# Remainders of the weights on VectorE: seven block products, the sums of their weights, and the order around the output projection

## The chip, the cores and the metric

The kernel runs on one core of one Trainium2 chip, in one launch. Its time is the device time of that launch in microseconds (us), and lower is better. "Before" is the kernel as it stood, "after" is the kernel with the change below; both compute the same outputs from the same inputs.

## The reference

One layer of a streaming encoder, on 1024 rows of 1024 columns, all in float32. Its parts, cut to what matters:

```python
mod = (silu(c) @ ada_w + ada_b)          # six vectors: shift, scale, gate, twice
h = rmsnorm(x, pre_norm_mix) * (1 + scale_m) + shift_m
q_lat, kv_lat, k_idx, w_idx, z, xbc, dt_raw, g_a, g_b = split(h @ w_in)
y_a = sparse_mla_attention(...) @ w_o_attn
y_b = ssd_mixer(z, xbc, dt_raw, ...) @ w_o_ssd          # 2048 -> 1024
mix = (sigmoid(g_a) * y_a + sigmoid(g_b) * y_b) @ w_out
x = x + gate_m * rmsnorm(mix, post_norm_mix)
h2 = rmsnorm(x, pre_norm_ffn) * (1 + scale_f) + shift_f
u_gate, u_up = split(h2 @ w_ffn_in)                     # 2 x 2816 columns
x = x + gate_f * rmsnorm((silu(u_gate) * u_up) @ w_ffn_out, post_norm_ffn)
```

ssd_mixer is a Mamba-2 scan: a causal convolution of four taps over xbc, softplus of dt_raw, a scan in chunks, and at its end rmsnorm(y * silu(z), ssd_norm). sparse_mla_attention scores the keys with a small indexer, keeps the best 256, and attends to these.

## The kernel before

**Precision.** A float32 operand is used as two halves: "hi", a copy rounded to TensorE's fast float32 format (made by ScalarE, for weights at L155), and "lo", the remainder src - hi (for weights at L156, `wlo`). One product of 128x128 weights with 128x512 data is three matmuls: hi by hi, hi by lo, lo by hi. So every tile of weights costs one instruction of ScalarE and one subtraction, and TensorE waits for both.

**Weights.** `Stream W` brings them in tiles of 128x512 (four blocks of 128x128) in the order in which they are planned: a load on SP's queue into `wraw` (4 buffers), `whi` (3) and `wlo` (3). A tile is loaded and split two tiles ahead of its use. In before every `wlo` is made by GpSimd.

**Buffers.** Four arenas of 128x512 tiles: H (32), Q (26), R (8, of twice the size), EV (9). A tile is free when its last reader is done.

**Order.** The Tile scheduler orders the instructions of each engine by a simulated timeline; only in sections under `in_order` TensorE's order is that of the code. So an instruction that is handed to another engine, or written elsewhere, moves its neighbours on every engine.

**Stages**, in the time of the profiled execution: the projection w_in (from the start on, with the convolutions of xbc and the gates z), attention (660 to 1110 us lie wholly in it), the scan's end and the projection of attention, then the products of w_o_ssd (1437 to 1669 us, matmuls at L1625), w_out in two halves (L1416, ahead of the last products and behind them), and the feed-forward part (L1694 and on).

**The seven products.** w_o_ssd, 2048 by 1024, and the normed y are cut into 2x2 blocks, and the result is formed of seven products of half size in place of eight. `SEQ` and `SEQ1` list them as (i, c): product i (1 to 7) for column tile c (0 to 3), 24 matmuls each, two tiles of weights. Products 4 to 7 need sums of weight blocks. `ssd_sums` forms these ahead of time and stores them in DRAM (`d_s`): 8 units, each four loads, four additions or subtractions on GpSimd (L1029 to L1032) and four stores; before, they are called in the projection phase (`SUMS_AT`, and in the first two groups of the convolution), on four buffers `sum_bufs` (`adaw` and `vt` in the traces).

`ssd_step` runs one (i, c): its `tasks` first (sums of y: `both_sums`, `last_sum`, `third_sum`, `plain`), then 24 matmuls, then the addition of the result in PSUM (`pos`) to the partial sums. A sum of y is split by `y_parts` into `yh` (ScalarE) and `yw` (the remainder, L1258, or L1261 where it is scaled). `merge_out` joins a finished column tile with the gates in four steps: multiply by the gate (L1403), add the attention's part (L1404), hi (ScalarE, L1406), lo (L1407); w_out reads the result, `mg`. Rows of the output have two halves of 512, b = 0 and b = 1; `mixed(b)` is w_out for half b, eight column tiles of 24 matmuls. `residual_steps(0)`, the norm and residual of half 0 (`mix`, `sqm`, `xr`, h2), is spread over the last products and `mixed(1)`. Its row norms are L276 (spread by TensorE) and L270 (GpSimd).

Before, the order on TensorE is: 22 products, `mixed(0)`, six products, `mixed(1)`:

```python
SEQ = [(i, c) for i in (1, 2, 6, 5, 3) for c in range(4)] + [(7, 0), (7, 1)]
SEQ1 = [(4, 0), (7, 2), (4, 1), (7, 3), (4, 2), (4, 3)]
```

**Feed-forward.** `gate_up(t)` forms tile t of both halves of w_ffn_in, again by block products with weights' sums; `w_parts` splits a tile (ScalarE L1686, GpSimd L1687). The last two tiles before `EARLY` are "held": part of their work is done earlier and finished later; a rule of the code (`ends`) keeps one of these products behind another on TensorE.

**Attention's side work.** `ada_next()` is called again and again beside attention. It brings the columns of ada_w for the modulation vectors (two loads, then GpSimd's L326 and L327 on `adaw`) and a few late items. GpSimd also makes the masks `nm` there (L803) and `r` (L864).

## Time and profile before

| | |
|---|---|
| runs | 2388.24, 2385.63, 2382.94 us; median 2385.63 |
| profiled execution | 2381.24 us, its span 2379.5 us (1.7 us lie around it) |
| granted TensorE clock, mean | 0.990 |
| ScalarE, busy | 1217.8 us, 51% of the span |
| HBM | 304.84 MB read, 107.24 MB written, 173 GB/s over the span |
| GpSimd's `wlo` (L156) over the whole span | 238 instructions, 332.3 us, 1.40 us each |
| GpSimd's `wr` (L1687, two forms together) | 151 instructions, 217.9 us |
| between 660 and 1110 us: GpSimd's L803, L326, `wlo`, L327 | 74.7, 55.1, 36.5, 34.8 us |

How to read the rows that follow. The profile is of one execution on the chip. PE is TensorE's matmuls, PEld its weight loads, DVE is VectorE, ACT ScalarE, POOL GpSimd, SP the queue that issues DMAs. A row of a group names the line, the engine, the operation, what it writes and reads by the program's names, shapes, and the count; then busy time and the mean of one in ns; then idle time of the engine just ahead, and what ended it. A row of the instructions in time begins with the start and the duration in us. A row of waits reads: engine, its instruction, `<-` the instruction or DMA that released it, and total us, times, longest. "PEclk" is the granted clock as a share of full speed.

### The profile page before, as it was taken

The numbers are of one execution on the slowest core, as the hardware profiler recorded it, in microseconds if no ns is written. First come the engines' busy times: TensorE is split into PE (matmuls) and PEld (weight loads), VectorE is DVE, ScalarE is ACT, GpSimd is POOL, SyncE is SP. The second block draws the span as 40 slices with busy tenths as digits, with TensorE's granted clock in tenths as the row PEclk, the third lists the DMA queues.
The fourth block names the chain that finished last, engine by engine and source line by source line (L and its number), as shares of the span: only waits on it lengthen the run. The fifth ranks groups of instructions, "written<-read, shape, count | busy, mean of one in ns | idle before, by whom it ended". The sixth has DMA issues, their size and how long they took to land. (4 is left out here: it accounts for less than half of the span.)

```text
span 2379.5 us, 35122 instructions
## 1 busy us (share of the span) xinstructions
PE 2317.4 (97%) x11736; PEld 1893.8 (80%) x11736; DVE 1650.6 (69%) x3040; ACT 1217.8 (51%) x2362; POOL 1233.2 (52%) x947
## 2 busy tenths in 40 slices
PE   9999999999999999999999998999999999999997
PEld 5878888888888888888887776788788788888886
...
GB/s 268 153 232 247 195 174 163 196 89 97 99 80 85 98 89 100 98 90 144 224 239 287 292 251 281 211 176 208 89 274 137 132 161 149 162 94 282 208 194 165
DMA packets 251716, 411.27 MB, mean 173 GB/s; under 512 B 25568, under 2 KB 93328, under 8 KB 251536
## 3 DMA queue, kind: packets, MB, share of 16 engines
...
HBM read 304.84 MB, written 107.24 MB: 173 GB/s over the span
## 5 line engine op out<-in xcount | busy, mean ns | idle before, releaser
L156 POOL TENSOR_TENSOR wlo<-wraw,whi 128x512 fp32r<-128x512 f32 x238 | 332.3, 1399 | 371.4 <-ACT whi L155 340.8
L1694 PE MATMUL p<-xh,wr 128*128 128x512 f32 x880 | 273.6, 391 | 3.2 <-DVE g L1785 3.0
L155 ACT ACTIVATE whi<-wraw 128x512 fp32r<-128x512 f32 x238 | 148.7, 627 | 211.8 <-issue 52.5
L1687 POOL TENSOR_TENSOR wr<-a,wr 128x512 fp32r<-128x512 f32 x107 | 153.7, 1451 | 94.1 <-ACT wr L1686 61.9
L1694 PEld LDWEIGHTS p<-xh,wr 128*128 128x128 f32 x880 | 165.9, 189 | 38.5 <-DVE g L1785 3.4
L1694 PE MATMUL p<-xl,wr 128*128 128x512 f32 x440 | 171.8, 390 | 0.0
L252 POOL TENSOR_TENSOR fwl<-fw,fwh 128x512 fp32r<-128x512 f32 (+1 forms) x78 | 108.2, 1398 | 103.1 <-ACT fwh L251 70.5
L326 POOL TENSOR_TENSOR adaw<-adaw,cs 128x512 f32<-128x512 f32 x64 | 68.1, 1065 | 153.2 <-DMA adaw<-ada_w 116.5
L856 ACT ACTIVATE lg<-lg,mx 128x256 f32<-128x256 f32 (+7 forms) x128 | 99.1, 774 | 57.4 <-DVE mx L853 57.2
L1686 ACT ACTIVATE wr<-a 128x512 fp32r<-128x512 f32 x107 | 65.9, 628 | 114.5 <-PE p L1694 84.4
L651 DVE SCALAR_TENSOR_TENSOR acc<-rel,widx,acc 128x384 f32<-128x384 f32 (+2 forms) x90 | 106.7, 1208 | 15.2 <-ACT rel L646 14.9
L1694 PE MATMUL p<-h2h,wr 128*128 128x512 f32 x352 | 110.4, 391 | 1.7 <-ACT xh L251 1.4
L701 ACT ACTIVATE junk<-acc,cand__2216 128x1024 bf16<-128x1024 f32 (+2 forms) x96 | 86.3, 898 | 39.5 <-DVE cand__2216 L744 31.2
L646 ACT ACTIVATE rel<-prel 128x512 f32<-128x512 f32 (+3 forms) x160 | 77.0, 523 | 45.9 <-PE prel L645 42.6
L1625 PE MATMUL pos<-yh,wlo 128*128 128x512 f32 x224 | 90.2, 403 | 8.7 <-POOL wlo L156 8.6
L1694 PEld LDWEIGHTS p<-xl,wr 128*128 128x128 f32 x440 | 83.0, 189 | 17.3
L1687 POOL TENSOR_TENSOR wr<-s,wr 128x512 fp32r<-128x512 f32 x44 | 64.2, 1463 | 61.0 <-ACT wr L1686 56.2
L1625 PE MATMUL pos<-yh,whi 128*128 128x512 f32 x224 | 90.1, 402 | 1.4 <-ACT whi L155 1.0
L699 DVE TENSOR_SCALAR_CACHE_REDUCE junk<-acc,cand__2225 128x896 bf16<-128x896 f32 (+2 forms) x96 | 88.5, 922 | 1.5
L1625 PE MATMUL pos<-yw,whi 128*128 128x512 f32 x224 | 89.1, 398 | 0.0
L853 DVE CUSTOM_DVE_ANT_0 lg<-plg,nm 128x256 f32<-128x256 f32 (+1 forms) x128 | 51.5, 404 | 52.9 <-PE plg L844 52.3
L1416 PE MATMUL pot<-mg,whi 128*128 128x512 f32 x256 | 80.6, 396 | 3.6 <-ACT whi L155 3.4
...
## 6 DMA issues: line engine op xcount, KB each, us to landing
wraw<-w_in SPq DMA_DIRECT2D x129, 256.0 KB, 2.8
a<-w_ffn_in SPq DMA_DIRECT2D x122, 256.0 KB, 3.2
al<-d_a SPq DMA_DIRECT2D x88, 256.0 KB, 4.3
yl<-d_y SPq DMA_DIRECT2D x72, 256.0 KB, 3.9
adaw<-ada_w SPq DMA_DIRECT2D x64, 256.0 KB, 2.9
...
d_a<-g SPq DMA_DIRECT2D x42, 256.0 KB, 2.3
...
```

The costliest lines, as they stand in the source:

```text
L155: self.hi = behind(S.activation(hi[:, :kt], raw[:, :kt], AF.Copy))
L156: self.lo = behind(G.tensor_tensor(lo[:, :kt], raw[:, :kt], f(hi[:, :kt]), op=OP.subtract))
L252: (lo_eng or V).tensor_tensor(lo, src, f(hi), op=OP.subtract)
L646: S.activation(rel[:, 512 * b:512 * b + w_], pr[:, 0:w_], AF.Relu)
L651: V.scalar_tensor_tensor(acc[i][:, 0:n], rel[:, 0:n], ws, acc[i][:, 0:n], op0=OP.mult, op1=OP.add)
L699: V.tensor_scalar(jk, y, a_, 0.0, op0=op, op1=OP.add, accum_out=o)
L701: S.activation(jk, y, AF.Sign, scale=-1.0, bias=a_, accum_out=o)
L856: S.activation(lg[:, 0:n], lg[:, 0:n], AF.Exp, scale=-1.0, bias=m, accum_out=rr[:, 2 * t + hh:2 * t + hh + 1])
L1416: T.matmul(o, wt[:, k % 4, :], xs[k][xi][0], start=first and n == 0 and i == 0, stop=last and n == len(ks) - 1 and i == 2)
L1625: T.matmul(p, w[k // 4][wi][:, k % 4], YO[i][k][xi], start=start and k == 0 and n == 0, stop=k == SK - 1 and n == 2, skip_group_check=True)
L1687: G.tensor_tensor(w[:, 1], src, f(w[:, 0]), op=OP.subtract)
L1694: ins.append(T.matmul(p, w[:, wi, i], X[x][i][xi], start=start and i == 0 and k == 0, stop=i == 3 and k == 2, skip_group_check=True).ins)
```

## The change

1. **Remainders of weights.** `Stream W` gets a list of engines, `eng`. It is GpSimd as before, VectorE while `SEQ` runs, and from the first w_out on VectorE and GpSimd by turns.
2. **Sums and merges of the products.** The remainders of y for products 3 and 5, the subtraction in `third_sum`, and the addition in `merge_out` are all on VectorE; before, GpSimd had some or all of them.
3. **Products ahead of w_out.** `SEQ` now has 26 products, `SEQ1` two. Six merges of half 1 are done by `merge_later` during `mixed(0)`, with buffers of H and Q; the last two follow their products. `residual_steps(0)` is handed out in other places, and one multiply-add of h2 goes to ScalarE.
4. **Sums of the weights.** `ssd_sums` becomes a generator, called from `ada_next()`: a step is one instruction of GpSimd with its store, a unit has three EV tiles (`wsum`), and all of it lies beside attention. The projections no longer have it.
5. **Feed-forward.** `w_parts` of the two held tiles are on VectorE, and the rule `ends` is dropped.

```diff
         def load(self):
...
-            self.lo = behind(G.tensor_tensor(lo[:, :kt], raw[:, :kt], f(hi[:, :kt]), op=OP.subtract))
+            self.lo = behind(self.eng[len(self.tiles) % len(self.eng)].tensor_tensor(lo[:, :kt], raw[:, :kt], f(hi[:, :kt]), op=OP.subtract))
...
     def ada_next():
+        next(sums, None)
...
+    def ssd_sums():
+        for c in range(4):
+            for k0 in (0, 4):
+                x, y, z = (EV("wsum", (P, 4, P)) for _ in range(3))
...
+                load(x, c, 0)
+                load(y, 4 + c, 0)
+                load(z, 4 + c, SK)
+                yield
+                G.tensor_tensor(x, y, x, op=OP.subtract)
+                store(0, x)
+                yield
+                G.tensor_tensor(y, z, y, op=OP.subtract)
+                store(2, y)
+                yield
+                G.tensor_tensor(z, x, z, op=OP.subtract)
+                store(1, z)
+                load(x, c, SK)
+                yield
+                G.tensor_tensor(x, x, z, op=OP.add)
+                store(3, x)
...
     def conv_group(g):
...
-            elif g or i > 1:
-                ssd_sums(*next(s_units))
...
-    def merge_out(t, b, src, sb, ld, eng=V):
+    def merge_out(t, b, src, sb, ld, where=None):
         V.tensor_tensor(sb, src, sb, op=OP.mult)
-        eng.tensor_tensor(sb, sb, ld, op=OP.add)
-        hi, lo = in_r("mg")
+        V.tensor_tensor(sb, sb, ld, op=OP.add)
+        hi, lo = (where("mg", dt=F32R), where("mg", dt=F32R)) if where else in_r("mg")
...
+            if b == 0:
+                behind_merge(S.activation(h2, h2, AF.Identity, bias=mod[:, 24 + t:25 + t], scale=am2[:, t:t + 1]))
+            else:
+                behind_merge(V.tensor_scalar(h2, h2, am2[:, t:t + 1], mod[:, 24 + t:25 + t], op0=OP.mult, op1=OP.add))
...
-    SEQ = [(i, c) for i in (1, 2, 6, 5, 3) for c in range(4)] + [(7, 0), (7, 1)]
-    SEQ1 = [(4, 0), (7, 2), (4, 1), (7, 3), (4, 2), (4, 3)]
+    SEQ = [(i, c) for i in (1, 2, 6, 5, 3, 7) for c in range(4)] + [(4, 0), (4, 1)]
+    SEQ1 = [(4, 2), (4, 3)]
...
-            y_parts(5, k, y21, H_, eng=G)
+            y_parts(5, k, y21, H_)
...
-            y_parts(3, k, s2, H_, eng=(V, G)[k % 2])
+            y_parts(3, k, s2, H_)
...
-            (G if k % 2 else V).tensor_tensor(x[0], x[0], x[1], op=OP.subtract)
+            V.tensor_tensor(x[0], x[0], x[1], op=OP.subtract)
...
+    def merge_later(t):
+        x = merge_in(t, 1)
+        merge_gate(1, x[0])
+        merge_out(t, 1, u4s[t - 4] if t > 3 else u2s[t], *x, where=Q if t > 3 else H_)
...
+        W.eng[:] = [V]
         for n, x in enumerate(SEQ):
             ssd_step(x, (SEQ + SEQ1)[n + 1])
...
-        out = []
+        out, W.eng[:] = [], [V, G]
         for t, _ in enumerate(mixed(0, MG[0], out)):
-            load, work = next(plains)
-            work(load())
+            if t < 6:
+                merge_later((4, 5, 6, 7, 0, 1)[t])
         rest = residual_steps(0, *out, x1, 2)
         for n, x in enumerate(SEQ1):
             ssd_step(x, (SEQ1 + [None])[n + 1])
-            if n < 4:
-                next(rest)
+            next(rest)
         out = []
         for t, _ in enumerate(mixed(1, MG[1], out)):
-            if t in (0, 2, 3):
+            for _ in range((3, 0, 1, 1, 0, 0, 0, 0)[t]):
                 next(rest)
...
+        parts_eng[0] = V if t in held else G
...
-        if t == EARLY - KEPT + 1:
-            tc.add_manual_dep(ends[0], j.name, mybir.DependencyInfo(
```

After's lines are numbered 14 to 16 higher in this part of the code: L1258 is L1272, L1403 to L1407 are L1417 to L1421, L1642 is L1657.

Where the instructions stand on an engine, at three places. A row has the line, the operation and what it writes from what it reads, with the buffers' numbers. The first is GpSimd at the start of the products (1437 us in before). `zy` is the last product of y with the gate z; `wlo` and `yw` are remainders of weights and of y. Before:

```order
L1226 TENSOR_TENSOR zy_14693<-zy_14693 128x512
L156 TENSOR_TENSOR wlo_14881<-wraw_14879,whi_14880 128x512
L156 TENSOR_TENSOR wlo_14922<-wraw_14920,whi_14921 128x512
L1258 TENSOR_TENSOR yw_14954<-yl_14936,yh_14953 128x512
L1258 TENSOR_TENSOR yw_15020<-yl_14961,yh_15019 128x512
L156 TENSOR_TENSOR wlo_14928<-wraw_14926,whi_14927 128x512
L1258 TENSOR_TENSOR yw_15089<-yl_15027,yh_15088 128x512
L156 TENSOR_TENSOR wlo_14971<-wraw_14969,whi_14970 128x512
L156 TENSOR_TENSOR wlo_15037<-wraw_15035,whi_15036 128x512
L1258 TENSOR_TENSOR yw_15161<-yl_15096,yh_15160 128x512
L156 TENSOR_TENSOR wlo_15043<-wraw_15041,whi_15042 128x512
```

After the change, GpSimd at the same place (`wlo_16391` is a weight of w_out, 26 products on):

```order
L1240 TENSOR_TENSOR zy_14717<-zy_14717 128x512
L156 TENSOR_TENSOR wlo_14905<-wraw_14903,whi_14904 128x512
L156 TENSOR_TENSOR wlo_14946<-wraw_14944,whi_14945 128x512
L156 TENSOR_TENSOR wlo_14952<-wraw_14950,whi_14951 128x512
L270 TENSOR_TENSOR r_15033<-v_15031,nhalf_96 128x4
L270 TENSOR_TENSOR r_15174<-v_15172,nhalf_96 128x4
L156 TENSOR_TENSOR wlo_16391<-wraw_16389,whi_16390 128x512
```

And VectorE after the change, a little later in the same section (`yl` and `s2` are sums of y, `ya` the attention's projection):

```order
L1321 SCALAR_TENSOR_TENSOR ya_14909<-ya_14909,poa_14911 128x512
L1272 TENSOR_TENSOR yw_15113<-yl_15051,yh_15112 128x512
L156 TENSOR_TENSOR wlo_14995<-wraw_14993,whi_14994 128x512
L1272 TENSOR_TENSOR yw_15109<-s2_15105,yh_15108 128x512
L1275 SCALAR_TENSOR_TENSOR yw_15117<-yl_15057,vec_87,yh_15116 128x512
L1560 SCALAR_TENSOR_TENSOR yl_15120<-yl_15122,vec_87,yl_15120 128x512
L156 TENSOR_TENSOR wlo_15061<-wraw_15059,whi_15060 128x512
L1566 TENSOR_TENSOR s2_15105<-yh_14750,yl_15120 128x512
L1272 TENSOR_TENSOR yw_15185<-yl_15120,yh_15184 128x512
```

The remainders of weights and of y have left GpSimd's row and stand between VectorE's own sums of y.

The second place is VectorE after the last product, up to the last remainder of a merge (`mg`), which the second w_out needs last. `mk4` is that product's sum; `mix` and `xr` belong to the norm and residual of half 0. Before:

```order
L1469 TENSOR_TENSOR mix_16510<-mix_16510,mix_16462 128x512
L1404 TENSOR_TENSOR sgb_16761<-sgb_16761,yal_16762 128x512
L1469 TENSOR_TENSOR mix_16558<-mix_16558,mix_16510 128x512
L1407 TENSOR_TENSOR mg_16862<-sgb_16761,mg_16862 128x512
L1642 TENSOR_TENSOR mk4_14932<-pos_16777,mk4_14932 128x512
L1403 TENSOR_TENSOR sgb_16819<-mk4_14932,sgb_16819 128x512
L1404 TENSOR_TENSOR sgb_16819<-sgb_16819,yal_16820 128x512
L1407 TENSOR_TENSOR mg_16905<-sgb_16819,mg_16905 128x512
```

VectorE after the change, the rows that end with the last `mg`:

```order
L1417 TENSOR_TENSOR sgb_16790<-mk4_14956,sgb_16790 128x512
L1478 SCALAR_TENSOR_TENSOR mix_16636<-mix_16636,gm_14938,prn_16888 128x512
L1478 SCALAR_TENSOR_TENSOR mix_16689<-mix_16689,gm_14938,prn_16888 128x512
L1478 SCALAR_TENSOR_TENSOR mix_16742<-mix_16742,gm_14938,prn_16888 128x512
L1478 SCALAR_TENSOR_TENSOR mix_16784<-mix_16784,gm_14938,prn_16888 128x512
L1479 TENSOR_TENSOR xr_16895<-mix_16477,xr_16895 128x512
L1479 TENSOR_TENSOR xr_16899<-mix_16583,xr_16899 128x512
L1418 TENSOR_TENSOR sgb_16790<-sgb_16790,yal_16791 128x512
L1479 TENSOR_TENSOR xr_16907<-mix_16689,xr_16907 128x512
L1483 TENSOR_TENSOR mix_16477<-mix_16477,mix_16425 128x512
L156 TENSOR_TENSOR wlo_16957<-wraw_16955,whi_16956 128x512
L1421 TENSOR_TENSOR mg_16885<-sgb_16790,mg_16885 128x512
```

The four steps of the last merge stood together; now steps of the residual and a remainder of w_out's weights stand between them, five more instructions ahead of L1417 (four of `mix`, one of `wlo`) not shown.

The third place is GpSimd in the first projections, with the weights' sums in before (L1029 to L1032):

```order
L156 TENSOR_TENSOR wlo_3178<-wraw_3176,whi_3177 128x512
L1029 TENSOR_TENSOR adaw_2831<-adaw_2832,adaw_2831 128x512
L1030 TENSOR_TENSOR adaw_2832<-vt_2833,adaw_2832 128x512
L1031 TENSOR_TENSOR vt_2833<-adaw_2831,vt_2833 128x512
L270 TENSOR_TENSOR r_858<-v_856,nhalf_96 128x4
L1032 TENSOR_TENSOR vt_2833<-vt_2833 128x512
L156 TENSOR_TENSOR wlo_3184<-wraw_3182,whi_3183 128x512
L156 TENSOR_TENSOR wlo_3269<-wraw_3267,whi_3268 128x512
```

After the change these sums stand on GpSimd beside attention (L1039 to L1049), among the masks and the columns of ada_w:

```order
L326 TENSOR_TENSOR adaw_7123<-adaw_7123,cs_134 128x512
L327 TENSOR_TENSOR adaw_7122<-adaw_7122,adaw_7123 128x512
L1039 TENSOR_TENSOR wsum_6950<-wsum_6951,wsum_6950 128x512
L156 TENSOR_TENSOR wlo_7032<-wraw_7030,whi_7031 128x512
L1042 TENSOR_TENSOR wsum_6951<-wsum_6952,wsum_6951 128x512
L326 TENSOR_TENSOR adaw_7279<-adaw_7279,cs_134 128x512
L1045 TENSOR_TENSOR wsum_6952<-wsum_6950,wsum_6952 128x512
```

A unit's four instructions have moved from one run in the projections to single places beside attention, each behind its own loads.

More of the change, by code (lines that the diff above doesn't have):

```diff
@@ L44 @@
 SK = 8
-SUMS_AT = range(2)
 COLS = {}
@@ L142, in __init__ @@
             self.tag, self.width, self.bufs = tag, width, (raw_bufs, hi_bufs, lo_bufs)
+            self.eng = [G]
         def plan(self, items):
@@ L1019, in weight_sums, with load, store @@
             SP.dma_start(d_t[i, c][:, k0:k0 + n], x)
-    s_units = iter([(c, k0) for c in range(4) for k0 in (0, 4)])
-    def ssd_sums(c, k0):
-        b11, b12, b21, b22 = sum_bufs
-        for x, t, o in ((b11, c, 0), (b12, 4 + c, 0), (b22, 4 + c, SK), (b21, c, SK)):
-            tc.add_manual_dep(SP.dma_start(x, a["w_o_ssd"][t][:, o + k0:o + k0 + 4]).ins, W.issue, mybir.DependencyInfo(
-                mybir.DependencyClass.NoSync, mybir.DependencyReason.DATA), reason="behind")
-        G.tensor_tensor(b11, b12, b11, op=OP.subtract)
-        G.tensor_tensor(b12, b22, b12, op=OP.subtract)
-        G.tensor_tensor(b22, b11, b22, op=OP.subtract)
-        G.tensor_tensor(b21, b21, b22, op=OP.add)
-        for i, x in enumerate((b11, b22, b12, b21)):
-            SP.dma_start(d_s[i, c][:, k0:k0 + 4], x)
+    def ssd_sums():
+        for c in range(4):
+            for k0 in (0, 4):
+                x, y, z = (EV("wsum", (P, 4, P)) for _ in range(3))
+                def load(d, t, o):
+                    tc.add_manual_dep(SP.dma_start(d, a["w_o_ssd"][t][:, o + k0:o + k0 + 4]).ins, ada_after[0], mybir.DependencyInfo(
+                        mybir.DependencyClass.NoSync, mybir.DependencyReason.DATA), reason="behind")
+                def store(i, d):
+                    SP.dma_start(d_s[i, c][:, k0:k0 + 4], d)
+                load(x, c, 0)
[14 more added lines that the diff above has]
+                store(3, x)
+    sums = ssd_sums()
     def conv_group(g):
-        for i, t in enumerate(group_tiles(g)):
+        for t in group_tiles(g):
             conv_out(conv(*t))
@@ L1600, in build @@
         tasks[3, c] = [third_sum(5 + c, H_)] * (c < 3) + [gates_of(4 + c, 0)]
-        tasks[7, c] = [gates_of(4 + c, 1)]
-        tasks[4, c] = [gates_of(c, 1)]
-    plains = iter([plain(4, k, 1) for k in range(SK)])
+        tasks[7, c] = [plain(4, 2 * c, 1), plain(4, 2 * c + 1, 1)]
+        tasks[4, c] = [] if c < 2 else [gates_of(c, 1)]
     loaded = {}
@@ L1636, in ssd_step @@
         elif i == 3:
-            merge_out(4 + c, 0, p, *gates[4 + c, 0], eng=G)
+            merge_out(4 + c, 0, p, *gates[4 + c, 0])
         elif i == 7:
             V.tensor_tensor(u4s[c], p, u4s[c], op=OP.add)
-            merge_out(4 + c, 1, u4s[c], *gates[4 + c, 1], eng=G)
         else:
             V.tensor_tensor(u2s[c], p, u2s[c], op=OP.add)
-            merge_out(c, 1, u2s[c], *gates[c, 1])
+            if c > 1:
+                merge_out(c, 1, u2s[c], *gates[c, 1])
+    def merge_later(t):
+        x = merge_in(t, 1)
+        merge_gate(1, x[0])
+        merge_out(t, 1, u4s[t - 4] if t > 3 else u2s[t], *x, where=Q if t > 3 else H_)
     def ry(b):
@@ L1682, in w_load @@
         return r
+    parts_eng = [G]
     def w_parts(src):
@@ L1686, in w_parts @@
         S.activation(w[:, 0], src, AF.Copy)
-        G.tensor_tensor(w[:, 1], src, f(w[:, 0]), op=OP.subtract)
+        parts_eng[0].tensor_tensor(w[:, 1], src, f(w[:, 0]), op=OP.subtract)
         return w
     def product(p, w, x, start):
-        ins = []
         for i in range(4):
             for k, (wi, xi) in enumerate(P3):
-                ins.append(T.matmul(p, w[:, wi, i], X[x][i][xi], start=start and i == 0 and k == 0,
-                                    stop=i == 3 and k == 2, skip_group_check=True).ins)
-        return ins
+                T.matmul(p, w[:, wi, i], X[x][i][xi], start=start and i == 0 and k == 0, stop=i == 3 and k == 2,
+                         skip_group_check=True)
     def first_two(a11, a12):
@@ L1706, in first_two @@
         return p, p1, p2
-    held, lower_n, sum_n, ahead, ends = {}, [0], [0], [None], [None]
+    held, lower_n, sum_n, ahead = {}, [0], [0], [None]
     def sum_tile(name):
@@ L1786, in gate_up @@
         p5 = bank("p5")
-        j = product(p5, w_parts(s1), "1", True)[-1]
-        if t == EARLY - KEPT + 1:
-            tc.add_manual_dep(ends[0], j.name, mybir.DependencyInfo(
-                mybir.DependencyClass.NoSync, mybir.DependencyReason.DATA), reason="behind")
+        product(p5, w_parts(s1), "1", True)
         u1 = EV("u1")
@@ L1804, in gate_up @@
         SP.dma_start(d_a[t][:, half(1)], g1)
-        ends[0] = product(p, w_parts(a22), "4", False)[0]
+        product(p, w_parts(a22), "4", False)
         if p1 is None:
```

3 lines of the change are left out of this document (removed).

## The prediction

> **What bounds the kernel now.** I read the page first, then the busy times by stage, the engines' waits, and single instructions in time.
>
> ```profile
> span 2379.5 us, 35122 instructions
> PE 2317.4 (97%) x11736; PEld 1893.8 (80%) x11736; DVE 1650.6 (69%) x3040; ACT 1217.8 (51%) x2362; POOL 1233.2 (52%) x947
> ```
>
> TensorE (PE) is busy 97% of the span, so only what makes it wait, or run at a lower clock, can be won. The view by stretches (busy us, instructions begun, granted clock, DMA share) says where that is:
>
> ```profile
> core 0: us, PE busy (x) PEld busy (x) DVE busy (x) ACT busy (x) POOL busy (x), PEclk, DMA share, GB/s
> ...
> 160.00:180.00 20.00, 14.91 (x59) 11.96 (x58) 13.92 (x25) 5.15 (x7) 10.57 (x8) 0.83 0.62 223
> ...
> 660.00:1110.00 450.00, 446.06 (x2879) 371.91 (x2879) 315.59 (x932) 243.71 (x502) 220.34 (x211) 1.00 0.28 91
> ...
> 1437.00:1530.00 93.00, 79.24 (x325) 61.29 (x324) 88.60 (x81) 42.38 (x77) 68.88 (x44) 0.94 0.79 257
> 1530.00:1633.00 103.00, 103.00 (x456) 85.27 (x456) 38.01 (x40) 44.83 (x77) 58.95 (x45) 1.00 0.49 162
> 1633.00:1669.00 36.00, 35.23 (x158) 28.05 (x156) 30.11 (x36) 15.49 (x27) 26.62 (x19) 1.00 0.69 246
> 1669.00:1722.00 53.00, 47.96 (x205) 38.20 (x206) 32.51 (x40) 24.25 (x43) 30.09 (x22) 0.97 0.27 90
> ...
> 1820.00:1880.00 60.00, 55.40 (x235) 44.72 (x234) 40.12 (x43) 21.02 (x38) 38.11 (x27) 0.97 0.39 126
> ```
>
> The fed stretch 1530 to 1633 gives TensorE's pace: 103/456 = 0.226 us a matmul. Against it (length minus count times 0.226) the others lose: 160-180 (call it C) 6.7 us; 1437-1530 (A, the first products) 19.6; 1633-1669 0.3; 1669-1722 (B, the second w_out) 6.7; 1820-1880 (E, the first feed-forward tiles) 6.9. The change touches the causes of all of them; together they are 40 us. TensorE's own waits there (total, times, longest):
>
> ```profile
> PE pos L1625 <- POOL wlo L156: 8.6, 8, 2.1
> PE prn L276 <- POOL r L270: 3.5, 1, 3.5
> ...
> PE pot L1416 <- ACT whi L155: 3.4, 2, 2.9
> ...
> PE p L1694 <- DVE g L1785: 3.0, 1, 3.0
> ...
> PE pw L231 <- DVE cv L988: 5.6, 3, 5.1
> ```
>
> In A, TensorE waits for remainders of weights (wlo) that GpSimd (POOL) makes; in C for a convolution tap of VectorE (DVE). Why are they late? Instructions in time around 1445, 1486 and 1536:
>
> ```profile
> 1445.18 0.69 DVE L1550 TENSOR_TENSOR s<-yw,s 128x512 f32<-128x512 f32 x1
> 1445.78 0.69 DVE L1258 TENSOR_TENSOR yw<-s,yh 128x512 fp32r<-128x512 f32 x1
> ...
> 1485.32 1.75 DVE L1258 TENSOR_TENSOR yw<-s,yh 128x512 fp32r<-128x512 f32 x1
> 1486.99 1.77 DVE L1562 SCALAR_TENSOR_TENSOR s<-yl,vec,s 128x512 f32<-128x512 f32 x1
> 1488.69 1.77 DVE L1258 TENSOR_TENSOR yw<-s,yh 128x512 fp32r<-128x512 f32 x1
> ...
> 1497.12 0.68 DVE L1630 TENSOR_TENSOR vt<-pos,vt 128x512 f32<-128x512 f32 x1
> ...
> 1486.48 1.73 POOL L1258 TENSOR_TENSOR yw<-yl,yh 128x512 fp32r<-128x512 f32 x1
> 1488.17 1.74 POOL L1258 TENSOR_TENSOR yw<-s,yh 128x512 fp32r<-128x512 f32 x1
> ...
> 1536.01 1.30 POOL L156 TENSOR_TENSOR wlo<-wraw,whi 128x512 fp32r<-128x512 f32 x1 [1.43 <-ACT whi L155]
> ```
>
> VectorE's remainder (L1258) takes 0.69 us and follows its neighbour by 0.60 at 1445, but 1.75 to 1.77 with starts 1.70 apart at 1486, where GpSimd works at the same step: 1.69 apart and 1.73 each, against 1.30 alone. The two take turns: a turn of 1.70 holds one VectorE instruction (0.61) and one of GpSimd (so 1.09). L1630, with one input in PSUM, takes 0.68 while GpSimd works. GpSimd's work in A, by groups:
>
> ```profile
> L156 POOL TENSOR_TENSOR wlo<-wraw,whi 128x512 fp32r<-128x512 f32 x26 | 40.3, 1559 | 17.0 <-ACT whi L155 15.5 <-issue 1.4
> L1258 POOL TENSOR_TENSOR yw<-yl,yh 128x512 fp32r<-128x512 f32 x8 | 13.2, 1670 | 2.0 <-ACT yh L1257 2.0
> L1258 POOL TENSOR_TENSOR yw<-s,yh 128x512 fp32r<-128x512 f32 x4 | 6.6, 1639 | 2.9 <-DMA wraw<-d_s 2.9
> L1570 POOL TENSOR_TENSOR yl<-yl 128x512 f32<-128x512 f32 x3 | 4.9, 1649 | 1.4 <-DMA yl<-d_y 1.4
> ...
> L1226 POOL TENSOR_TENSOR zy<-zy 128x512 f32<-128x512 f32 x1 | 1.7, 1678 | 1.4 <-PE poa L241 1.4
> ```
>
> That is 42 instructions at 1.09, 45.8 us, and 81 of VectorE at 0.61, 49.4: 95 us for a stretch of 93. So A is bound by the two engines' turns.
>
> **The change, part by part.**
>
> *A: remainders, sums and merges of the products on VectorE.* By the order, GpSimd keeps four or five of the 42 (the last z product and the first wlo); 37 go to VectorE. New: 5 x 1.09 + (81 + 37) x 0.61 = 77.4 us instead of 93, a gain of 15.6. TensorE needs 325 x 0.226 = 73.4, so the rest is nearly balanced. VectorE idles 4.4 us in A today, and a remainder that follows its ScalarE half at once will wait some tenths: I take 1.6 off, **14 us**. Bounds: at most 19.6 (TensorE never waits); at least about 8, if each of the 37 saves 0.22, less than half of the worked 0.48 (1.09 - 0.61). wlo now stands in VectorE's queue behind sums that wait for their loads, and TensorE waits for it; it is made two tiles before use, 24 matmuls or 5.4 us, more than the 3.9 in which a yl lands (row under D).
>
> The Trainium skill, page "SBUF — State Buffer", section "Who interferes with whom", says that a VectorE instruction with two SBUF inputs and a GpSimd one that reads SBUF exclude each other, one blocking until the other is done. The trace agrees that they exclude each other (1.75 against 0.69) but not with the whole length: 1.30 + 0.69 would give a turn of 1.99, and it is 1.70. By the rule each moved instruction saves 0.61 to 0.69, 37 of them over 22 us, and A would gain its cap, 19.6.
>
> *Products moved ahead.* Four products, (7,2), (7,3), (4,0), (4,1), go ahead of the first w_out with their weights: TensorE's count is the same, their loads and ScalarE halves too. They fall in the fed stretch, where VectorE is busy 38 of 103 us; with all 45 of GpSimd's instructions there at 0.61 it would have 38 + 27 = 65. The 38 us left are the cover, so **0**. If it were gone, each further remainder would cost 0.61 us.
>
> *B.* What is left after the last product is one merge, but in after's order its four steps stand among eight mix, three xr and two wlo instructions:
>
> ```profile
> 1646.62 3.37 DVE L1464 SCALAR_TENSOR_TENSOR mix<-mix,gm,prn 128x512 f32<-128x512 f32 x5
> ...
> 1675.70 0.68 DVE L1642 TENSOR_TENSOR mk<-pos,mk 128x512 f32<-128x512 f32 x1
> ...
> 1678.96 0.69 DVE L1407 TENSOR_TENSOR mg<-sgb,mg 128x512 fp32r<-128x512 f32 x1 [0.70 <-ACT mg L1406]
> ```
>
> Now the last merge ends at 1679.7, 11 us after the last product (1668.6), since VectorE is 7 us behind. After: 9 instructions reading PSUM at 0.67 (3.37/5) and 9 others at 0.61, 11.5 us, plus about three turns of GpSimd's xr and wlo at 1.09: 14.8 us. TensorE has 42 matmuls that don't need it, 9.5 us; it waits 5.3, and restarts at a lower clock (C below: 1.6). Sum 6.9 against 6.7 lost now: **0**, from 4 worse (four instructions of GpSimd's, 1.09 each, put in front of the merge) to 6.7 better.
>
> *C: the weights' sums leave the first projections.* The chain that TensorE waits 5.1 us for:
>
> ```profile
> 158.19 0.42 DVE L556 TENSOR_TENSOR dt_tmp<-dt_tmp 128x256 f32<-128x256 f32 x1
> 158.64 1.40 DVE L557 TENSOR_TENSOR dt_tmp<-dt_tmp 128x256 f32<-128x256 f32 x1
> 160.08 1.27 DVE L558 TENSOR_SCALAR dt_tmp<-dt_tmp 128x256 f32<-128x256 f32 x1
> 161.38 3.24 DVE L560 SCALAR_TENSOR_TENSOR dt_tmp<-dt_tmp 128x256 f32<-128x256 f32 x5
> ...
> 156.88 1.29 POOL L1031 TENSOR_TENSOR vt<-adaw,vt 128x512 f32<-128x512 f32 x1
> 158.25 1.52 POOL L1032 TENSOR_TENSOR vt<-vt 128x512 f32<-128x512 f32 x1
> ```
>
> At 0.42 each these seven save 1.0 + 0.85 + 1.1 = 3 us, if GpSimd is out of the way: its sums are, its wlo aren't. The loss of 6.7 is 5.1 of wait and 1.6 of clock (0.83 in the stretch). I take 3 and most of the clock: **4.5 us**; between 0 and 6.7.
>
> *D: the same sums beside attention.* 8 units of four GpSimd instructions, four loads and four stores. They are 32 x 1.30 = 42 us on a GpSimd that has 230 of 450 us free there; SP's queue carries 64 more transfers, and a unit holds three of nine EV buffers. GpSimd's waits there (total, times, longest), and the landing of such a 256 KB load:
>
> ```profile
> POOL adaw L326 <- DMA adaw<-ada_w: 103.1, 43, 6.2
> ```
>
> ```profile
> yl<-d_y SPq DMA_DIRECT2D x72, 256.0 KB, 3.9
> ```
>
> GpSimd already stands 103 us behind 43 loads there and TensorE loses 3.9 of 450: 0.09 a load. I charge half of that for each of the 32 loads, **1.5 us**; between 0 (hidden) and 8, two such loads' landing uncovered in full (3.9 x 2).
>
> *E: halves of two feed-forward tiles on VectorE, an ordering rule dropped.* Ten remainders move; the wait there is for g (L1785), made by VectorE behind a load, before and after. **0**, between 3 worse and 3 better (that one wait of 3.0, gone or doubled). The residual's ScalarE form of h2 has ScalarE half idle (24.25 of 53): nothing.
>
> Sum: 14 + 0 + 4.5 - 1.5 + 0 = 17 us. The profiled execution took 2381.24, so 2364.2; the runs' median, 2385.63, lies 4.4 above it, and against that it is 2368.6. I predict **2368 us**.
>
> **Rivals.**
> 1. *Everything that was lost in A is won, TensorE is the bound*, since the turns vanish: A 19.6, C 6.7, B 3, less 1.5: 28 us, 2358. For it: the 77.4 and 73.4 are near. Against: the first wlo stand behind some 20 VectorE instructions. By the rule of the Trainium skill's page "SBUF — State Buffer" above, this is the case to expect.
> 2. *Transfers become the bound in A.* It moves 257 GB/s x 93 us = 23.9 MB at a DMA share of 0.79; at share 0.95 that is 77 us, at 0.9 82: gain 11 and less, about 8 with late loads in front of VectorE's queue. Sum 11, 2375.
> 3. *The change doesn't do what it says:* VectorE, with all of it in one queue, stays late, and B gets worse by 4: A 6, C 2, D 3: 1 us, 2385. Against: the 0.69 and 1.75 of the same line.
> 4. *Slower: the sums block attention.* A GpSimd wsum that waits for its load stands ahead of r and wlo, which TensorE needs. 32 instructions at 1.3 and 8 landings of 3.9 are 73 us; half of it uncovered costs 36, net 18 worse (36 against the 18.5 of the other terms), 2403. It decides from 0.6 us of uncovered wait per instruction (18.5/32). Against: the 103 us of such waits without harm.
>
> **How the numbers follow.** The likeliest case, gain 12 to 22, has 0.47; rival 1 0.15; rival 2 0.2; rival 3 0.1; rival 4 0.08. Leaving out rivals 3 and 4, with rival 1 and 2 taken out to gains of 31 (A, C and B in full, less 2) and 6, the range is 2354 to 2380. A change of 0.2% is 4.8 us, about what a measurement can tell: faster 0.82 (the first three cases), same 0.10, slower 0.08.
>
> **What would show it.** In the changed profile VectorE's L1272 and wlo should take 0.6 to 0.7 us through the products and GpSimd be nearly idle; TensorE's waits for POOL wlo there vanish and DVE wlo takes their place with a few us; the time from the first product to where TensorE is fed (1437 to 1530 now) shortens by 14. At the RECIPROCAL the five dt_tmp steps take under 2.4 us and the wait for cv is 2 us. After the last product a wait of about 5 us for mg remains. The forecast is wrong if VectorE's two-input instructions stay near 1.7, if PE waits appear between 660 and 1110, or if DMA shares reach 0.95 in A with VectorE idle.

## The result and the profile after

After took 2365.11 us in the median of 4 runs (2363.40 to 2366.18), before 2386.64 of 4 (2382.94 to 2388.24): a ratio of 0.9911, 95% interval 0.9894 to 0.9928, 21.5 us faster. The forecast was 2368. The profiled executions lie 17.8 us apart (2381.24 and 2363.40): before's lies 5.4 under the median of its runs, after's 1.7. So stages compared between the two traces add up to 17.8 and not to 21.5.

The page of after, the span and the engines:

```profile
span 2361.7 us, 35083 instructions
PE 2310.4 (98%) x11736; PEld 1892.1 (80%) x11736; DVE 1651.2 (70%) x3134; ACT 1224.0 (52%) x2370; POOL 1076.2 (46%) x845
```

VectorE has 94 instructions more than before and is no busier (1651.2 against 1650.6 us), and GpSimd has 157 us less. The stretches of after (busy us, instructions begun, granted clock, DMA share, GB/s), with the products cut at their 264th matmul (11 products) and their 528th:

```profile
core 0: us, PE busy (x) PEld busy (x) DVE busy (x) ACT busy (x) POOL busy (x), PEclk, DMA share, GB/s
160.00:180.00 20.00, 19.10 (x91) 15.56 (x90) 14.95 (x26) 11.47 (x17) 13.28 (x10) 1.00 0.71 261
660.00:1110.00 450.00, 444.31 (x2897) 370.28 (x2896) 313.56 (x940) 248.13 (x512) 256.55 (x241) 1.00 0.41 131
1442.40:1510.10 67.70, 65.67 (x288) 52.98 (x289) 65.25 (x104) 39.74 (x69) 7.40 (x4) 0.97 0.92 312
1510.10:1572.00 61.90, 60.51 (x266) 49.45 (x265) 37.76 (x59) 27.45 (x47) 0.00 (x0) 1.00 0.62 196
1649.00:1705.50 56.50, 51.80 (x220) 41.76 (x218) 37.34 (x49) 35.66 (x60) 29.41 (x22) 0.94 0.45 146
1800.00:1860.00 60.00, 56.64 (x247) 46.24 (x246) 44.61 (x50) 22.90 (x41) 29.16 (x19) 0.99 0.36 120
```

The same two cuts in before:

```profile
1447.10:1529.80 82.70, 70.44 (x288) 54.94 (x289) 79.04 (x69) 38.25 (x69) 64.57 (x41) 0.94 0.78 255
1529.80:1589.40 59.60, 59.60 (x264) 49.35 (x264) 21.27 (x22) 22.85 (x38) 36.56 (x28) 1.00 0.53 175
```

In the first 11 products VectorE went from 69 instructions in 79.04 us to 104 in 65.25. One group shows how, the scaled remainder of y, which the change did not touch (busy, mean ns of one): the same six instructions take less than half of their time. Before:

```profile
L1261 DVE SCALAR_TENSOR_TENSOR yw<-yl,vec,yh 128x512 fp32r<-128x512 f32 x6 | 10.2, 1694 | 0.4 <-ACT yh L1260 0.4
```

and after:

```profile
L1275 DVE SCALAR_TENSOR_TENSOR yw<-yl,vec,yh 128x512 fp32r<-128x512 f32 x6 | 4.4, 740 | 0.0
```

By the starts of the same matmuls in the two traces, the time went like this (us):

| stretch | before | after | difference |
|---|---|---|---|
| start to the first indexer score | 200.4 | 192.1 | -8.3 |
| to the last attention score | 908.9 | 910.9 | +2.0 |
| to the first product | 337.8 | 339.4 | +1.6 |
| first 11 products | 82.7 | 67.7 | -15.0 |
| next 11 | 59.6 | 61.6 | +2.0 |
| to the 1000th feed-forward matmul | 370.0 | 370.0 | 0 |
| to the last matmul | 411.2 | 411.2 | 0 |

A second trace of after (run 8 below) shows how far one such row can be trusted: 193.9, 913.3, 341.3, 68.9, 62.0, 366.4 and 410.3 us. The two zeros, the +2.0 of attention and the +1.6 lie within what the same kernel gives twice; the -8.3, the -15.0 and the +2.0 of the next 11 products don't.

### The profile page after: what moved, and what is told of

The parts are those of the page before. It is cut to its first block, busy times and chain, and to the rows that moved or that the text cites. A ratio compares the mean times of both kernels' runs of the same rounds, so it can differ in the third digit from the quotient of the medians.

```text
span 2361.7 us, 35083 instructions
## 1 busy us (share of the span) xinstructions
PE 2310.4 (98%) x11736; PEld 1892.1 (80%) x11736; DVE 1651.2 (70%) x3134; ACT 1224.0 (52%) x2370; POOL 1076.2 (46%) x845
## 3 DMA queue, kind: packets, MB, share of 16 engines
HBM read 304.84 MB, written 107.24 MB: 174 GB/s over the span
## 5 line engine op out<-in xcount | busy, mean ns | idle before, releaser
L156 POOL TENSOR_TENSOR wlo<-wraw,whi 128x512 fp32r<-128x512 f32 x170 | 233.3, 1373 | 494.0 <-ACT whi L155 462.1
L1711 POOL TENSOR_TENSOR wr<-a,wr 128x512 fp32r<-128x512 f32 x102 | 146.3, 1448 | 94.8 <-ACT wr L1710 64.5
L1711 POOL TENSOR_TENSOR wr<-s,wr 128x512 fp32r<-128x512 f32 x40 | 57.6, 1442 | 77.1 <-ACT wr L1710 72.0
L877 PE MATMUL pt<-ident,lg 128*128 128x128 f32 x576 | 82.3, 273 | 0.0
```

The source lines that it names most:

```text
L156: self.lo = behind(self.eng[len(self.tiles) % len(self.eng)].tensor_tensor(lo[:, :kt], raw[:, :kt], f(hi[:, :kt]), op=OP.subtract))
L877: T.transpose(ptv[:, hh, t, :], PR[hh, t][:, j * P:(j + 1) * P], ident)
L1711: parts_eng[0].tensor_tensor(w[:, 1], src, f(w[:, 0]), op=OP.subtract)
```

## The experiments

All ratios are to the kernel before, with the 95% interval.

**1. The weights' sums alone.** Part 4 of the change on the kernel before.

```diff
-            if t in SUMS_AT:
-                ssd_sums(*next(s_units))
...
     def ada_next():
+        next(sums, None)
```

> Before with one part of the change: the weights' sums (ssd_sums) beside attention instead of in the projections; all else as before. Between the traces of before and after, the same place was 8.3 us earlier at the end of the convolution's softplus (183.8 against 175.5), 6.3 at the end of attention's last scores (1109.3 against 1103.0) and 4.7 at the first product (1447.1 against 1442.4). Theory (the parts add up): this kernel is about 5 us faster than before, 0.998, with the wait for cv near 160 us gone and nothing gained in the products. Rival (the 1.6 us lost in attention and the 1.6 lost in the scan come from other changes of order): 8 us faster, 0.9965.

2382.49 us against 2386.99, ratio 0.9978 (0.9967 to 0.9988): 4.5 us, as the sum of the parts said. TensorE's wait for cv fell to 1.9 us, not to nothing, and the first 11 products took 82.6 us, as before. The stages of this one trace (196.7, 911.2 and 341.2 us) don't show the 4.5, so here are the means over all kernels run: to the first indexer score 203.0 us in the mean with the sums in the projections (4 kernels, 200.4 to 206.6) and 194.1 without (10 kernels, 192.1 to 197.8); attention 909.2 and 911.7; from there to the first product 338.9 and 340.6. That is -8.9, +2.5 and +1.8, together -4.6. In the first two the two sets don't overlap; in the third they do (337.8 to 340.5 against 339.1 to 343.1). The rival, that the two losses come from elsewhere, doesn't fit: both are there with nothing else of the change, and its 0.9965 lies just outside the interval.

**2. The engines alone.** Parts 1 and 2 on the kernel before, in its order of products.

```diff
+        W.eng[:] = [V]
         for n, x in enumerate(SEQ):
...
-            y_parts(5, k, y21, H_, eng=G)
+            y_parts(5, k, y21, H_)
```

> Before with the two parts that hand work from GpSimd to VectorE: remainders of weights on VectorE through the first products and by turns from the first w_out on, and the sums and merges of the products on VectorE. Products in the order of before, weights' sums in the projections, feed-forward as before. Theory (turns: GpSimd and VectorE exclude each other on SBUF, so what counts is how much GpSimd does there): the first 22 products take 129.5 us instead of 142.6, the whole is 11 to 15 us faster, 0.994 to 0.9955. Rival (the order: the gain of the products comes from the four products moved ahead of w_out): at most 4 us faster.

2370.86 us, ratio 0.9928 (0.9914 to 0.9941), 16 us faster, a little more than expected. The first 11 products:

```profile
1454.40:1522.10 67.70, 64.46 (x288) 51.68 (x289) 65.26 (x104) 39.92 (x69) 7.38 (x4) 1.00 0.91 310
```

The same 67.7 us as after, and the next 11 in 59.6. So the order is not what gained. 0.9978 x 0.9928 is 0.9906: runs 1 and 2 together give the whole change (0.9911), within the intervals.

**3. Unneeded work on GpSimd.** After, and for each tile that VectorE splits, the same remainder once more on GpSimd, into a tile that nothing reads.

```diff
             self.lo = behind(...)
+            if self.eng == [V]:
...
+                behind(G.tensor_tensor(self.spare[:, :kt], raw[:, :kt], f(hi[:, :kt]), op=OP.subtract))
```

> After, with unneeded work added on GpSimd: for every tile of weights that VectorE splits in the products (52), GpSimd forms the same remainder once more, into a tile that nobody reads. Nobody waits for it. Theory (turns): VectorE's remainders take 1.7 us again wherever GpSimd runs beside them; 22 to 24 of these fall where VectorE is 97% busy (1432 to 1480) and just behind, at 1.09 us each some 25 us of VectorE's time, of which the slack of the products up to 1560 takes up a half: 8 to 14 us slower than after, all of it in the first 22 products. Rival (latency: what mattered was that a remainder takes 0.68 us on VectorE and 1.3 to 1.7 on GpSimd, and that VectorE waits for nobody): within 2 us of after.

2390.61 us, ratio 1.0011 (1.0000 to 1.0022): 25 us slower than after, and no faster than before. Nobody waits for these instructions. The rival (latency) is out, and the theory's size was too small: I had counted on slack, and there was hardly any. The first 11 products, then the longest waits of TensorE in all the products (total, times, longest):

```profile
1447.30:1534.10 86.80, 72.37 (x289) 56.35 (x288) 86.58 (x103) 38.43 (x67) 43.25 (x26) 0.90 0.74 240
```

```profile
PE pos L1645 <- DVE wlo L156: 16.9, 9, 4.3
PE prn L280 <- POOL r L274: 3.2, 2, 2.8
```

VectorE took 86.58 us for 103 instructions, and TensorE stood behind VectorE's remainders. The second row is the norm of the rows of y, whose `r` GpSimd makes after a step of VectorE: TensorE waited 3.5 us for it in before, too, and in after not at all. VectorE itself waited for one thing only in these 86.8 us:

```profile
DVE wlo L156 <- ACT whi L155: 0.2, 1, 0.2
```

**4. Unneeded work, small.** The same 52 instructions on 128x4 elements.

```diff
-G.tensor_tensor(self.spare[:, :kt], raw[:, :kt], f(hi[:, :kt]), op=OP.subtract)
+G.tensor_tensor(self.spare[:, 0, 0:4], raw[:, 0, 0:4], f(hi[:, 0, 0:4]), op=OP.subtract)
```

> After, with the 52 unneeded instructions on GpSimd again, at the same places and waiting for the same halves of weights, but on 128x4 elements instead of 128x512. Theory (turns: what cost 25 us was the time for which GpSimd keeps VectorE from SBUF): within 4 us of after, the first 22 products in 129 to 133 us instead of 155.9. Rival (the 25 us came from GpSimd holding the buffers of the halves, since VectorE stood 9.1 us behind halves that ScalarE made late): 15 us or more slower than after again.

2367.01 us, ratio 0.9908 (0.9888 to 0.9928): as after. The first 11 products, and GpSimd's group in them:

```profile
1446.30:1515.50 69.20, 65.36 (x288) 51.44 (x289) 65.30 (x104) 39.98 (x69) 29.92 (x26) 1.00 0.85 285
```

```profile
L160 POOL TENSOR_TENSOR spare<-wraw,whi 128x4 fp32r<-128x4 f32 x22 | 23.7, 1079 | 34.4 <-ACT whi L155 26.7 <-issue 6.9 <-POOL r L274 0.4
```

VectorE is back at 104 instructions in 65.30 us, with as many GpSimd instructions beside it as in run 3, waiting for the same halves. So run 3's loss in the first 11 (19.1 us, against 1.5 here, where after itself differs by 1.2 between two traces) is the time in which GpSimd keeps VectorE out, not the buffers that it holds. The row of VectorE's waits in run 3 says the same: a held buffer would have left it idle, and it was idle for 0.2 us. One part was missed: in this profiled execution, the slowest of the four, the first 22 products took 136 us and not 129 to 133. The second 11 took 66.8 (after 61.6, run 3 68.9); VectorE stood 6.9 us behind one load of y there, so that part of run 3's loss isn't settled by this run.

**5 and 6. One half of the engines' part each.** The remainders of weights alone (5), the sums, remainders of y and merges alone (6).

```diff
+        W.eng[:] = [V]                        # 5 only
...
-            y_parts(5, k, y21, H_, eng=G)     # 6 only
+            y_parts(5, k, y21, H_)
```

> Before with the remainders of weights alone handed to VectorE (through the first products; by turns with GpSimd from the first w_out on); the remainders of y, third sums and additions of the merges stay on GpSimd where they were. With both, the first 22 products took 127.5 us instead of 142.6 and the whole was 0.9928 of before (about 17 us). Theory (turns): of the 37 instructions that left GpSimd at the start, about 22 are remainders of weights; VectorE's time there is (81 + 22) x 0.61 + 20 x 1.09 = 84.6 us instead of 95.2: the 22 products take about 133, 9 to 10 us less than before, the whole 0.9955 to 0.9965. Rival (latency: TensorE only ever waited for remainders of weights, and those are now quick): nearly all 15 us, 0.993 to 0.994.

> Before with the other half alone: the remainders of y for products 3 and 5, the third sums and the merges' additions on VectorE, the remainders of weights all on GpSimd as before. Theory (turns): about 15 instructions leave GpSimd at the start, VectorE's time there is (81 + 15) x 0.61 + 27 x 1.09 = 88 us instead of 95.2: the 22 products 5 to 7 us shorter, the whole 0.997 to 0.998. Rival (latency): TensorE waits for the remainders of weights, which stay on GpSimd, and VectorE has more to do: 0 to 2 us, 0.999 to 1.000.

2377.74 and 2379.21 us, both 0.9957 (0.9943 to 0.9970). The latency rival wanted nearly all for 5 and nothing for 6; it is refuted twice. Theory's range for the whole held for 5, but not where theory put it: the first 22 products took 139.0 us against 142.3 before, 3.3 less in place of 9 to 10, so that the 0.9957 was luck. In 6 they took 137.4, 4.9 less (5 to 7 expected), and the whole gained more than its 0.997. Where the rest of the two gains lies, one trace of each doesn't show. Of the first 11 products, 5:

```profile
1449.80:1528.30 78.50, 69.66 (x289) 55.13 (x290) 72.95 (x91) 39.11 (x70) 32.07 (x19) 0.93 0.82 278
```

and 6:

```profile
1452.60:1528.80 76.20, 68.30 (x288) 53.69 (x289) 70.72 (x82) 38.45 (x69) 39.41 (x26) 0.96 0.82 272
```

Now the prediction's sum, 0.61 us for each VectorE instruction and 1.09 for each of GpSimd's in the stretch, can be held against all of these:

| kernel | VectorE | GpSimd | by the sum | measured |
|---|---|---|---|---|
| before | 69 | 41 | 86.8 | 82.7 |
| run 5, weights only | 91 | 19 | 76.2 | 78.5 |
| run 6, y only | 82 | 26 | 78.4 | 76.2 |
| run 2, and after | 104 | 4 | 67.8 | 67.7 |
| run 3, unneeded work | 103 | 26 | 91.2 | 86.8 |
| run 8, fewer instructions | 100 | 3 | 64.3 | 66.0 |

It is within about 5% everywhere. The differences come out worse: against before the sum has 10.6 us for run 5, 8.4 for run 6 and 19.0 for run 2, where 4.2, 6.5 and 15.0 were measured, and 23.4 for run 3 against after, where it was 19.1. In runs 5 and 6 VectorE is idle for 5.5 us of the stretch (after: 2.5), which no sum of turns contains; so the two halves together gain less than both at once. The 1.09 is a price for 128x512: run 4, with 26 instructions of GpSimd, 22 of them small, would come to 91.8 by the sum, and took 69.2.

**7. Two products back.** After, with 24 products ahead of the first w_out and four behind it.

```diff
-    SEQ = [(i, c) for i in (1, 2, 6, 5, 3, 7) for c in range(4)] + [(4, 0), (4, 1)]
-    SEQ1 = [(4, 2), (4, 3)]
+    SEQ = [(i, c) for i in (1, 2, 6, 5, 3, 7) for c in range(4)]
+    SEQ1 = [(4, c) for c in range(4)]
...
-            if t < 6:
-                merge_later((4, 5, 6, 7, 0, 1)[t])
+            if t < 4:
+                merge_later(4 + t)
...
-            for _ in range((3, 0, 1, 1, 0, 0, 0, 0)[t]):
+            for _ in range((1, 0, 1, 1, 0, 0, 0, 0)[t]):
```

> After, with two products more behind the first w_out: SEQ has 24 products (1, 2, 6, 5, 3, 7), SEQ1 the four of product 4, whose merges follow them; four merges of half 1 beside w_out, the residual of half 0 handed out as one step behind each of the four products, then one at t = 0, 2 and 3. Theory (what after still loses between the last product and the feed-forward part, 67 of 73 us busy, comes from the residual's steps crowding the last merge): these 6 us shrink by 3 to 5, so 2 to 5 us faster than after. Rival (the loss is the chain of the residual itself or of the merge, whatever stands beside it): the same as after within 1.5 us, or slower.

2366.52 us, ratio 0.9911 (0.9894 to 0.9928): the 2 to 5 us are not seen, though an interval of 4 us to each side would hide the lower end. In the second w_out TensorE now waited for the last merge:

```profile
PE pot L1430 <- ACT mg L1420: 2.8, 1, 2.8
PE pot L1430 <- DVE mg L1421: 1.3, 1, 1.3
PE pot L1430 <- POOL wlo L156: 0.7, 1, 0.7
```

So the next run took what stood beside that merge away.

```diff
             ssd_step(x, (SEQ1 + [None])[n + 1])
-            next(rest)
+            for _ in range((1, 2, 2, 0)[n]):
+                next(rest)
...
-            for _ in range((1, 0, 1, 1, 0, 0, 0, 0)[t]):
+            for _ in range((0, 0, 1, 1, 0, 0, 0, 0)[t]):
```

> The version with 24 products ahead of the first w_out, with the residual of half 0 handed out so that nothing of it is left beside the last merge: its first step behind the first of the four last products, two groups each behind the second and third, none behind the fourth nor at the first tile of the second w_out; the last two steps at t = 2 and 3 as before. There TensorE waited 2.8 and 1.3 us for the last merge. Theory (the residual's steps crowd the last merge): these waits shrink to 1 us or less and the clock's halving there (3.4 us) goes: 3 to 5 us faster than that version, 0.989 to 0.9905 of before. Rival (the last merge is a chain of five instructions on two engines and late whatever stands beside it): no change, 0.9905 to 0.992.

2365.29 us, ratio 0.9902 (0.9887 to 0.9916): the same again. The waits moved:

```profile
PE pot L1430 <- POOL wlo L156: 2.8, 2, 1.7
PE pot L1430 <- DVE mg L1421: 1.2, 1, 1.2
PE pot L1430 <- ACT whi L155: 0.6, 1, 0.6
PE pot L1430 <- ACT mg L1420: 0.5, 1, 0.5
```

The last merge cost 1.7 us in place of 4.1, and GpSimd's remainders 2.8 in place of 0.7. The theory named the wait. Its gain isn't shown: 0.9902 is in its range, but the interval takes in the 0.9911 of the first version as well.

**8. Fewer instructions of VectorE.** After, with the first four sums s2 in one instruction from a y in place of two from its halves; run beside after itself.

```diff
-            if k < 4:
-                hi, lo = YO[1][k]
-                V.tensor_tensor(s2, f(hi), y21, op=OP.subtract)
-                V.tensor_tensor(s2, f(lo), s2, op=OP.add)
-            else:
-                V.scalar_tensor_tensor(...)
+            V.scalar_tensor_tensor(...)
...
-        return lambda: [y_raw(k, 1), y_raw(SK + k, 1)] + [y_raw(k, 0)] * (k > 3), work
+        return lambda: [y_raw(k, 1), y_raw(SK + k, 1)] + [y_raw(k, 0)], work
```

> After itself once more, on the same chip as the three that follow, so that they can be compared with it and not with the kernel before alone. Expected: 0.991 of before, and the first 11 products in 67 to 68 us again.

> After, with four instructions of VectorE less in the first products: in both_sums for k below 4 the sum s2 is formed in one instruction from a y that is loaded once more, in place of two from its halves that lie in SBUF. Four loads of 256 KB more. Theory (in after VectorE bounds the first products: 103 of its instructions at 0.61 and 4 of GpSimd's at 1.09 make 67.2 us, 67.5 were measured, and TensorE alone needs 59.7): 4 x 0.61 = 2.4 us off the first 11 products, 65 us, the whole 1 to 3 us faster than after. Rival (transfers bound them, at a DMA share of 0.93 between 1432 and 1480): four loads of 0.25 MB at 317 GB/s are 3.3 us more, so 0 to 3 us slower.

After again: 2366.15 us (2363.99 to 2368.28), ratio 0.9901 (0.9886 to 0.9916), 11 products in 68.9, a little over the 67 to 68. With fewer instructions: 2362.37 us (2359.71 to 2363.80), ratio 0.9884 (0.9866 to 0.9901). The runs of the two don't overlap, by 0.2 us; 3.8 us faster by the medians, the best of all kernels here. The intervals do overlap.

```profile
1443.30:1509.30 66.00, 63.60 (x289) 52.03 (x288) 61.94 (x100) 37.37 (x66) 5.34 (x3) 1.00 0.93 316
```

The stretch took 66.0 us; five traces with after's code in it gave 66.2 to 68.9 (67.8 in the mean), this one and run 10's, which has the same edit, 66.0 and 65.4. That is 2.1 us in the mean, near theory's 2.4, with one of the five almost as low as these two.

The rival was not tested, for the four loads more are not there. `[y_raw(k, 0)] * (k > 3)` calls `y_raw` first and then multiplies the list by 0 or 1, so before and after issue these loads too, and nobody reads them. The loads of y in the whole trace of after and of this run (count, size, median us to landing):

```profile
yl<-d_y SPq DMA_DIRECT2D x72, 256.0 KB, 4.5
yl<-d_y SPq DMA_DIRECT2D x72, 256.0 KB, 4.4
```

Both read 304.84 MB from HBM. What the run shows is that with the same transfers (20.9 MB in the stretch, 21.1 in after) and fewer instructions of VectorE the stretch is not longer, at a DMA share of 0.93 in place of 0.92. How near transfers are to being the next bound stays open.

**9. The feed-forward part undone,** and **10. runs 7 and 8 joined** (the later version of 7).

```diff
-        parts_eng[0] = V if t in held else G
...
+        if t == EARLY - KEPT + 1:
+            tc.add_manual_dep(ends[0], j.name, ...)
```

> After, with the feed-forward part of the change undone: remainders of the two held tiles on GpSimd, the ordering rule in place again. The gain of 1.5 us that the traces show there (from the first feed-forward tiles to the 1000th matmul) is either the change's or one execution's. Theory (that part is worth nothing, as was forecast): within 2 us of after. Rival (it is worth its 1.5 to 3 us): slower by so much.

> The version of the seventh run (24 products ahead of the first w_out, nothing of the residual beside the last merge) with the one-instruction sums of the tenth. Theory (the two save at different places and add up): 3 to 6 us faster than after, 0.9885 to 0.99. Rival (the place behind the products is bounded by chains, the start by transfers): the same as after within 2 us.

2366.43 us, 0.9902 (0.9884 to 0.9920): the feed-forward part is worth nothing that can be measured. The joined version: 2366.29 us, 0.9898 (0.9882 to 0.9913), the same as after, as the rival had it, and without run 8's 3.8 us; the start kept its gain (65.4 us for 11 products) and the rest gave it back. Why is not settled: its attention took 913.1 us, at the upper end of 910.3 to 913.3, and its last stretch (from the 1000th feed-forward matmul on) 412.6, 1.7 more than in run 8; the later version of run 7 had 412.3 there.

## Why the prediction was right, and where it was not

**A, 14 us: right, by its own mechanism.** The trace shows 15.0 in the first 11 products, 13.0 over 22. VectorE's remainders take what was forecast, and the one that ran beside GpSimd takes 1.69. VectorE's rows, then GpSimd's beside the first of them:

```profile
1442.61 1.69 DVE L1272 TENSOR_TENSOR yw<-s,yh 128x512 fp32r<-128x512 f32 x1
...
1450.26 0.68 DVE L1272 TENSOR_TENSOR yw<-yl,yh 128x512 fp32r<-128x512 f32 x1
1450.86 0.68 DVE L156 TENSOR_TENSOR wlo<-wraw,whi 128x512 fp32r<-128x512 f32 x1
```

```profile
1442.47 1.28 POOL L156 TENSOR_TENSOR wlo<-wraw,whi 128x512 fp32r<-128x512 f32 x1 [3.53 <-ACT whi L155]
```

TensorE's waits for remainders of weights in the products fell from 8.6 us to these, and the 3.5 us for r are gone:

```profile
PE pos L1641 <- DVE wlo L156: 2.7, 4, 0.9
PE pos L1641 <- POOL wlo L156: 0.7, 1, 0.7
```

Rival 1, that all of A's loss is won, didn't come: 15.0 of 19.6. VectorE is busy 65.25 of the 67.70 us, and TensorE 65.67, so both are nearly full. TensorE alone would need 62 to 63 us by an estimate from these traces: 264 matmuls at 0.226, and 24 short ones of the norms that are busy for 3.1. Rival 2, transfers, had at most 11 us; 15.0 came, at a DMA share of 0.92. It is ruled out as it was priced, not as the next bound. Rival 3 wanted 6 us in A, rival 4 some 36 us of uncovered waits beside attention, where 2.0 came.

What run 3 settles is that work of GpSimd on large SBUF tiles takes VectorE's time: 0.87 us for each of run 3's 22 instructions more (19.1/22). The Trainium skill, page "SBUF — State Buffer", section "Who interferes with whom", calls what the two engines share an exclusive lock; runs 3 and 4 agree with it (19.1 us for long instructions, 1.5 for as many short ones). That A stopped at 15.0 says nothing against its whole-length blocking, though the prediction put A at its cap by that rule: in the first 11 products after has 4 instructions of GpSimd left, and VectorE's own 104 at 0.61 are 63 us whatever one of GpSimd's costs. Against the whole length speaks the turn of 1.70 in place of 1.99 alone.

**Products ahead, 0: nearly.** The cover was there in the mean (VectorE 37.76 of 61.90 us busy) but not at each place: the next 11 products lost 2.0 us, 1.4 of it in TensorE's waits for remainders, and in run 2, without the move, none. The move is not the only way to lose there: runs 5 and 6, without it too, lost 1.0 and 1.7. In after the remainders stand in VectorE's queue behind gates that wait for their loads, the danger that was named and priced at nothing:

```profile
1556.50 0.68 DVE L156 TENSOR_TENSOR wlo<-wraw,whi 128x512 fp32r<-128x512 f32 x1
1559.08 0.69 DVE L1413 SCALAR_TENSOR_TENSOR sgb<-sgb,rys 128x512 f32<-128x512 f32 x1 [1.90 <-DMA sgb<-d_gb]
1559.69 0.68 DVE L1418 TENSOR_TENSOR sgb<-sgb,yal 128x512 f32<-128x512 f32 x1
1560.29 2.07 DVE L1275 SCALAR_TENSOR_TENSOR yw<-yl,vec,yh 128x512 fp32r<-128x512 f32 x3
1562.27 0.69 DVE L156 TENSOR_TENSOR wlo<-wraw,whi 128x512 fp32r<-128x512 f32 x1
```

**B and E, 0: right in the number, B not in its mechanism.** From the 22nd product to the 1000th feed-forward matmul it is 370.0 us both times (366.4 in the second trace of after, so this zero is good to some 4 us), and run 9 gave nothing. B was to trade today's loss for a wait of 5 us for the last mg. That wait didn't come; 0.9 of it stayed, and others came, which add up to as much (5.7 with these four), so that the 0 was luck:

```profile
PE p L265 <- DVE mix L1483: 2.4, 1, 2.4
PE pot L1430 <- POOL wlo L156: 1.4, 1, 1.4
PE p L265 <- DVE sqm L1454: 1.0, 1, 1.0
PE pot L1430 <- DVE mg L1421: 0.9, 1, 0.9
```

**C, 4.5 us: mis-sized, and its step was wrong.** It gave 8.3 (8.9 in the mean), beyond the upper end of 6.7. The step "seven instructions at 0.42 each save 3 us" failed: L557 saved its 1.0 us (0.43 in place of 1.40), but the five L560 take 3.28 us after, 3.24 before, with a remainder of GpSimd still beside them (from 157.56 on), and L561 and L563 beside a feed-forward sum and another remainder take 1.43 and 1.34, before 0.70 and 0.43. What changed is when the chain begins. After:

```profile
151.75 1.74 DVE L555 RECIPROCAL dt_tmp<-dt_tmp 128x256 f32<-128x256 f32 x1
...
156.31 3.28 DVE L560 SCALAR_TENSOR_TENSOR dt_tmp<-dt_tmp 128x256 f32<-128x256 f32 x5
...
167.16 1.34 DVE L563 SCALAR_TENSOR_TENSOR dt<-dt_tmp 128x256 f32<-128x256 f32 x1
```

and before:

```profile
156.41 1.74 DVE L555 RECIPROCAL dt_tmp<-dt_tmp 128x256 f32<-128x256 f32 x1
...
171.88 0.43 DVE L563 SCALAR_TENSOR_TENSOR dt<-dt_tmp 128x256 f32<-128x256 f32 x1
```

It is as long (15.4 and 15.5 us) and begins 4.7 earlier. The bound of 6.7 was taken from 160 to 180 alone, while the sums ran from 80 us on: between 80 and 160 TensorE was busy for 78.6 us before, and for all 80 after and in run 1. What held the start of the chain back is not shown by a run of its own. TensorE's wait for cv there, 5.6 us before:

```profile
PE pw L231 <- DVE cv L989: 0.9, 1, 0.9
```

**D, -1.5: right in the number** (-2.0, and -2.5 in the mean of kernels). Its mechanism, a price per load of the sums, isn't shown: TensorE's waits between 660 and 1110 us grew from 3.6 to 5.8, all of them for VectorE and none for GpSimd or a load. Not foreseen at all was the stretch behind it, attention's end to the first product, 1.8 us longer in the mean where the sums have moved, though they are finished by then. The two sets overlap there, and the cause stays open.

So the total held partly by luck, since errors nearly cancel in the trace: C was 3.8 too small and A 1.0, and 2.0 and 1.6 us of loss (the next 11 products, the stretch after attention) were not in the sum. The 17.8 us of the traces are near the 17; the 21.5 of the medians are 4.5 more, and no term of the sum has these.
